# Issuing eleven of the bulk loads from ScalarE's DMA queue instead of SyncE's

## The chip, the cores and the metric

The kernel runs on one core of a Trainium2 chip. The metric is the device time of one execution in microseconds (us). A time is the median of the runs of that kernel; beside it stands the kernel before, run on the same chip in the same rounds. Of the engines only three matter: SyncE (SP in the profile) and ScalarE (ACT), which issue DMA transfers here and do nothing else, and VectorE (DVE), which does all the arithmetic.

## The reference

```python
x = np.random.randn(8192, 8192).astype(np.float32)
return np.linalg.norm(x, ord=np.inf, axis=1)      # the largest |x| of each row
```

268 MB are read once and 8192 numbers are written.

## The kernel before

48 of each partition's 64 rows are loaded in 24 bulk loads of two rows for each of the 128 partitions (64 KB a partition, 8.39 MB a load). Three buffers take turns, so load n+3 waits until reduction n has read its buffer. The last 16 rows, the tail, come in 31 smaller loads. I count loads and reductions from 0 throughout: the twelve loads of the first half are 0 to 11.

```python
    sbuf = ctx.enter_context(tc.tile_pool(name="sbuf", bufs=BUFS))     # BUFS = 3
    # ... (cut)
    def absmax(o, i):
        nc.vector.reduce_max(out=o, in_=i, axis=X, apply_absolute_value=True)

    for a in range(A):                       # A = 6
        for n in range(G):                   # G = 4: 24 bulk loads
            t = sbuf.tile([P, W + PAD], F32, tag="t")          # W = 16384
            nc.sync.dma_start(out=t[:, :W], in_=x_b[a, n])
            absmax(
                r_bulk[:, a, n * B : (n + 1) * B],
                t[:, :W].rearrange("p (b c) -> p b c", b=B),
            )
    nc.scalar.dma_start(out=out_b, in_=r_bulk[:])
    # ... (cut: the tail, 31 loads on nc.sync, each reduced as it lands)
    nc.at_finalize(start_first_load_early)   # SyncE's first load goes ahead of the start barrier
```

## Time and profile before

| | before |
|---|---|
| time, median of 3 | 628.22 us |
| span of the profiled run | 626.0 us |
| DVE busy | 552.9 us (88%) |
| read from HBM (the chip's main memory) | 268.44 MB, 429 GB/s over the span |

From the profile page of the kernel before, parts 1 and 2 (in the rows of digits each digit is the busy share of one fortieth of the span, in tenths):

```profile
span 626.0 us, 199 instructions
DVE 552.9 (88%) x64; POOL 0.2 (0%) x4
DVE  0588988889988889888898888988889999999998
DMA  9999999999999999999999999999999999999997
```

The DMA engines are busy in every slice. DVE has a little room until the last quarter, and almost none after it.

The timeline of the kernel before, cut to the start, the middle and the end of the bulk (start, duration, engine, line, operation, count; in brackets the idle time before it and what ended it):

```profile
22.00 17.22 DVE L139 TENSOR_REDUCE r_bulk<-t 128x2 f32<-128x16384 f32 x1 [21.02 <-DMA t<-in_x_dram]
41.27 17.22 DVE L139 TENSOR_REDUCE r_bulk<-t 128x2 f32<-128x16384 f32 x1 [2.06 <-DMA t<-in_x_dram]
...
234.67 17.22 DVE L139 TENSOR_REDUCE r_bulk<-t 128x2 f32<-128x16384 f32 x1 [2.14 <-DMA t<-in_x_dram]
254.02 17.22 DVE L139 TENSOR_REDUCE r_bulk<-t 128x2 f32<-128x16384 f32 x1 [2.13 <-DMA t<-in_x_dram]
273.32 17.22 DVE L139 TENSOR_REDUCE r_bulk<-t 128x2 f32<-128x16384 f32 x1 [2.07 <-DMA t<-in_x_dram]
292.69 17.22 DVE L139 TENSOR_REDUCE r_bulk<-t 128x2 f32<-128x16384 f32 x1 [2.15 <-DMA t<-in_x_dram]
...
466.68 17.22 DVE L139 TENSOR_REDUCE r_bulk<-t 128x2 f32<-128x16384 f32 x1 [2.14 <-DMA t<-in_x_dram]
```

A reduction starts every 19.33 us ((466.68 − 22.00) / 23), takes 17.22 us, and is preceded by about 2.1 us of waiting for its load. So the pace is that of the loads: 8.39 MB in 19.33 us, 434 GB/s.

From the same profile, the longest wait of SyncE's own queue (us in total, times, longest), the issue of load 14 in the timeline, and two lines of the DMA issues (the last number is the median time from issue to landing):

```profile
SPq L144 <- DVE r_bulk L139: 361.6, 21, 17.2
...
251.92 0.33 SPq L144 DMA_DIRECT2D t<-in_x_dram  x1
...
t<-in_x_dram SPq DMA_DIRECT2D x24, 40.7
out_dram<-r_bulk ACTq DMA_DIRECT2D x1, 24.0 KB, 60.4
```

SyncE mostly waits for buffers. A load is issued 21.4 us before the load ahead of it has landed (load 14: issued at 251.92, load 13 landed at 273.29), so it queues behind a whole load before it moves (the first packet of load 14 starts at 272.11). I call this time the **lead** of a load: from its issue to the landing of the load ahead of it. The store of r_bulk is only 24 KB but needs 60.4 us to land: on every engine its 48 packets of 32 B stand between packets of the loads, nearly all of them one at a time (in the order of the packet records, read as described below).

### The profile page before, as it was taken

To read this page: it belongs to the slowest core of one execution; us is meant where nothing else is said; L and a number is where in the kernel's file an instruction comes from. 1 tells how busy PE (TensorE), PEld (TensorE's weight loads), DVE (VectorE), ACT (ScalarE), POOL (GpSimd) and SP (SyncE) were. 2 spreads that over 40 slices of the span, in tenths; PEclk is the share of its full clock that TensorE was granted. 3 is DMA by queue.
4 is the path that set the end of the run, shared out by engine and by line. 5 is a ranking of instruction groups with operands and counts; after the bars stand their busy time and mean duration, and the time that the engine had idled before them with its cause. 6 is when DMAs were issued, how large, how long until landed. Compare 5 with 4: busy or idle time off the path is not lost.

```text
span 626.0 us, 199 instructions
## 1 busy us (share of the span) xinstructions
DVE 552.9 (88%) x64; POOL 0.2 (0%) x4
## 2 busy tenths in 40 slices
DVE  0588988889988889888898888988889999999998
POOL 0000000000000000000000000000000000000000
DMA  9999999999999999999999999999999999999997
GB/s 402 469 402 452 419 452 419 452 419 448 423 435 435 427 444 410 461 402 469 402 469 402 469 402 465 406 452 419 452 422 410 443 432 430 423 431 426 427 424 308
DMA packets 8994, 268.49 MB, mean 429 GB/s; under 512 B 1952, under 2 KB 1952, under 8 KB 3104
## 3 DMA queue, kind: packets, MB, share of 16 engines
q1 hardware_dynamic: 8064, 268.44, 99.4%
q10 hardware_dynamic: 928, 0.03, 0.1%
q14 instruction: 2, 0.02, 0.0%
HBM read 268.44 MB, written 0.03 MB: 429 GB/s over the span
## 4 chain that ended last, share of the span: by engine, by line
DMA 67%; DVE 29%; another core or an unknown queue 4%; SPq 0%; issue 0%
DMA t<-in_x_dram 67%; DVE r_bulk L139 22%; DVE part L139 5%; DVE t L139 1%; DVE r_fin L139 0%; SPq L157 0%; DVE r_tail L139 0%
## 5 line engine op out<-in xcount | busy, mean ns | idle before, releaser
L139 DVE TENSOR_REDUCE r_bulk<-t 128x2 f32<-128x16384 f32 x24 | 413.3, 17220 | 69.6 <-DMA t<-in_x_dram 69.6
L139 DVE TENSOR_REDUCE part<-t 128x1 f32<-128x8192 f32 (+18 forms) x31 | 130.4, 4274 | 0.8 <-DMA t<-in_x_dram 0.6
L139 DVE TENSOR_REDUCE t<-t 128x1 f32<-128x1152 f32 (+3 forms) x6 | 7.9, 1387 | 0.0
L139 DVE TENSOR_REDUCE r_fin<-t 128x1 f32<-128x1030 f32 x1 | 1.2, 1227 | 0.0
L136 DVE MEMSET part<- 128x60 f32 x1 | 0.1, 108 | 0.9 <-PEq L194 0.9
L139 DVE TENSOR_REDUCE r_tail<-part 128x15 f32<-128x60 f32 x1 | 0.2, 216 | 0.0
L194 POOL MEMSET const-uint8-127<- 128x1 uint8 x1 | 0.1, 102 | 0.0
L194 POOL MEMSET const-bfloat16-1.0<- 128x1 bf16 x1 | 0.1, 101 | 0.0
L194 POOL MEMSET const-float32-0.0<- 128x1 f32 x1 | 0.1, 98 | 0.2 <-issue 0.2
L194 POOL MEMSET const-float32-1.0<- 128x1 f32 x1 | 0.1, 98 | 0.0
## 6 DMA issues: line engine op xcount, KB each, us to landing
t<-in_x_dram SPq DMA_DIRECT2D x1, 6720.0 KB, 40.4
t<-in_x_dram SPq DMA_DIRECT2D x2, 3264.0 KB, 26.2
t<-in_x_dram SPq DMA_DIRECT2D x3, 2048.0 KB, 28.7
t<-in_x_dram SPq DMA_DIRECT2D x1, 6144.0 KB, 40.6
t<-in_x_dram SPq DMA_DIRECT2D x1, 5760.0 KB, 35.3
t<-in_x_dram SPq DMA_DIRECT2D x3, 1664.0 KB, 32.2
t<-in_x_dram SPq DMA_DIRECT2D x2, 2432.0 KB, 32.4
t<-in_x_dram SPq DMA_DIRECT2D x1, 4352.0 KB, 43.0
```

What stands on the lines that cost most here:

```text
L136: nc.vector.memset(part[:], 0.0)
L139: nc.vector.reduce_max(out=o, in_=i, axis=X, apply_absolute_value=True)
L194: nc = _bacc.Bacc("TRN2", target_bir_lowering=False, num_devices=1)
```

## The change

Issuing a DMA occupies a queue for about 0.33 us (0.328, the median of the 24 bulk loads before), and SyncE issues nearly all of them while ScalarE is idle. The intent is to share the issuing: loads 1 to 11 move to ScalarE; load 0 and everything from load 12 on stay on SyncE.

```diff
     for a in range(A):
         for n in range(G):
             t = sbuf.tile([P, W + PAD], F32, tag="t")
-            nc.sync.dma_start(out=t[:, :W], in_=x_b[a, n])
+            i = a * G + n
+            queue = nc.scalar if 1 <= i < A * G // 2 else nc.sync
+            queue.dma_start(out=t[:, :W], in_=x_b[a, n])
             absmax(
```

## The prediction

> **What bounds the kernel now.** The DMA engines. The DMA row of the page stands at 9 tenths in 39 of 40 slices, at 429 GB/s over the span. In the timeline the 24 bulk reductions start 19.33 us apart and take 17.22 us each; before each, DVE idles about 2.1 us. So a load of 8.39 MB takes 19.33 us (434 GB/s), and DVE has 2.1 us of slack per tile. SyncE's issue takes 0.33 us; its queue waits 361.6 us for DVE to free buffers. A load takes 40.7 us from issue to landing: it queues for about one whole load before it moves.
>
> **What the change does.** It saves SyncE 11 hidden issues: worth 0. It adds no bytes and no DVE work. It puts loads 1 to 11 (counting from 0) on a second ring. [...] the 24 KB store of r_bulk on ScalarE's queue, 48 packets per engine, took 60.4 us to land beside the loads, as if each packet waited for a load packet. So landings move in two places, where both rings hold loads:
>
> 1. Start. Load 0 is issued at 0.00 us, load 1 at about 0.8. Today load 0 lands at 22.0 and load 1 at 41.3. Now they alternate: load 0 lands at 36 to 41, load 1 still at 41. DVE begins some 17 us late. With 2.1 us of slack per tile it has caught up at about tile 8. Meanwhile loads are still issued 7 to 18 us before the previous one ends, so the engines stay fed.
>
> 2. Hand-over. Load 12 (SyncE) is issued when reduction 9 ends, about 213.2 us, and is ready as load 11 (ScalarE) begins to move, near 214.5. They share: both land near 251 to 254 instead of 234.7 and 254.0. Reduction 11 then ends at 269 to 271.5 and only then is load 14 issued, while load 13's last packets end at 272 to 273. An issue into idle engines needs 1.0 to 1.7 us to its first packet (load 0). So here the engines may run dry for 0 to 1 us: the only growth of the critical path. DVE catches up again by about tile 20, before the tail (466 us on), which is unchanged and has DVE at 9 tenths.
>
> **Time.** 628.2 + about 0.5 = 628.7 us; 8 in 10 between 627.8 and 630.5. Faster by over 2%: 0.01; within 2%: 0.97; slower: 0.02.
>
> **What would show it.** Right: total DVE busy unchanged (553 us), DMA row still 9 throughout at 428 to 429 GB/s; two DVE idles, about 38 us at the start (21.0 today) and 17 to 20 us before reduction 11, and then reductions back to back with no wait for some 8 tiles after each; reduction 23 starts within 1.5 us of 466.7. A lower DMA row or a DVE wait near 290 us would show the dry spell.
>
> **What would make it wrong.** Two rings at once moving less than one (over the 80 us where both are live, 3% is 2.4 us), or more; unequal sharing, which would starve load 11 past 254 us, and then load 14 is issued later and the engines idle for as long.

## The result, and the profile after

The changed kernel took 630.94 us (630.47 to 632.19, 6 runs) against 628.23 us (6 runs): a ratio of 1.0045, 95% interval 1.0032 to 1.0058. By the 2% rule that is the same; it is also 2.7 us slower, clear of noise, and above the predicted range. Ratios are the mean time of one kernel's fast runs over that of the other's of the same rounds, so not quite the ratio of the medians quoted.

The profile page of the changed kernel, the same lines:

```profile
span 628.3 us, 202 instructions
DVE 551.5 (88%) x64; POOL 0.2 (0%) x4
DVE  0059999999998880799999999988889999999998
DMA  9999999999999999999999999999999999999997
```

Its timeline, the same places:

```profile
0.80 194.13 ACTq L146 DMA_DIRECT2D t<-in_x_dram  x11
38.86 137.10 DVE L139 TENSOR_REDUCE r_bulk<-t 128x2 f32<-128x16384 f32 x8 [37.88 <-DMA t<-in_x_dram]
177.35 17.22 DVE L139 TENSOR_REDUCE r_bulk<-t 128x2 f32<-128x16384 f32 x1 [1.38 <-DMA t<-in_x_dram]
...
215.98 17.22 DVE L139 TENSOR_REDUCE r_bulk<-t 128x2 f32<-128x16384 f32 x1 [2.06 <-DMA t<-in_x_dram]
254.69 154.31 DVE L139 TENSOR_REDUCE r_bulk<-t 128x2 f32<-128x16384 f32 x9 [21.49 <-DMA t<-in_x_dram]
411.10 17.22 DVE L139 TENSOR_REDUCE r_bulk<-t 128x2 f32<-128x16384 f32 x1 [2.11 <-DMA t<-in_x_dram]
...
469.15 17.22 DVE L139 TENSOR_REDUCE r_bulk<-t 128x2 f32<-128x16384 f32 x1 [2.18 <-DMA t<-in_x_dram]
```

The course of events is the predicted one. DVE starts at 38.86 us instead of 22.00 and then makes eight reductions without a pause until it has caught up. It idles again for 21.49 us before reduction 11 (254.69 instead of 234.67) and catches up over nine more. But reduction 23 now starts at 469.15 instead of 466.68: 2.5 us have been lost, and not by DVE, which was waiting for loads again from 411 us on. The rows of tenths do not show the loss: the DMA row is the same digit for digit. The other sign that the prediction named, a wait of DVE near 290 us, does not appear either: DVE is still catching up then and reduction 13 starts at 288.95 us without a wait.

It has to be looked for at the hand-over. Load 14 waits for the buffer of load 11. In SyncE's part of the timeline it is issued at 271.94 us:

```profile
271.94 0.33 SPq L146 DMA_DIRECT2D t<-in_x_dram  x1
```

Load 13, ahead of it, landed at 273.96 by the trace's semaphore updates. So the lead of load 14 has shrunk from 21.4 us to 2.0.

The trace also records each DMA packet. A packet of a bulk load is 64 KB, as much as one partition gets; a load has 128, so 8 for each of the 16 engines, and one takes 2.418 us (median before). Chaining packets, each start to the end that it follows, gives for each engine the order of the packets of the two rings (by a ring I mean the packets of one queue at one engine; S: a packet of SyncE's ring, A: of ScalarE's). The chain is my own reading of the packet records, not a view of the profile:

```
first 41 us, all 16 engines:    S S A S A S A S A S A S A S A A A
                                load 0 is the eight S; the next A are load 1, the last begins load 2
from 215 us, 14 of 16 engines:  A S A S A S A S A S A S A S A S S
                                load 11 is the eight A; the first eight S are load 12, then load 13
load 11 on those engines:       last data packet ended 251.1 to 251.8 us
                                the 4-byte word that counts it as landed started 253.6 to 254.2 us
```

In these chains the rings take strict turns, one packet each. There is one thing in it that I had not reckoned with: a load has a packet of 4 bytes on its queue at each engine as well, after its data and 0.4 to 0.5 us ahead of one of the load's 16 semaphore updates (load 11). I take it for the word that raises the semaphore. In the chain it comes after one more packet of the other ring. All of load 11's data had been moved by 251.8 us, and on these engines the word started 2.4 us after the last packet; the last update came at 254.67, and DVE started at 254.69. Whether it was the turn that held the word, the traces do not tell.

Progress can be compared too: bytes moved up to a time, before minus after, divided by 434 GB/s. While two rings were live nothing was lost (0.05 us at 41 us; no growth from 214 to 254 us). The deficit grew by 0.7 us between 60 and 117 us, where packets took 2.44 to 2.57 us, by 0.8 us around 273 us, and by 0.3 us between 296 and 350 us, slow packets again. So the theory to test was: **the loss comes from load 14's short lead, not from having two rings.** The rivals were that two live rings move less; that moving work to ScalarE's queue costs in itself; and that DVE running without a pause slows the loads (the slow packets).

### The profile page after: what moved, and what is told of

Same layout as the page of the kernel before. It is cut to its first block, busy times and chain, and to the rows that moved or that the text cites. A ratio compares the mean times of both kernels' runs of the same rounds, so it can differ in the third digit from the quotient of the medians.

```text
span 628.3 us, 202 instructions
## 1 busy us (share of the span) xinstructions
DVE 551.5 (88%) x64; POOL 0.2 (0%) x4
## 4 chain that ended last, share of the span: by engine, by line
DVE 62%; DMA 32%; another core or an unknown queue 3%; issue 2%; SPq 0%
DVE r_bulk L139 47%; DMA t<-in_x_dram 32%; DVE part L139 14%; DVE t L139 1%; DVE r_fin L139 0%; SPq L159 0%; DVE r_tail L139 0%
```

## The experiments

All ran with 5 rounds. The diffs are against the changed kernel, or against the kernel before where said.

### 1. The change once more

No edit.

> The changed kernel once more, for a second trace and a narrower interval. In its first trace the lost time stood in three places: about 0.7 us of load progress between 60 and 117 us, where packets of 64 KB took 2.44 to 2.57 us instead of 2.418; 0.8 us at 273 us, where load 14 was issued 2.0 us before load 13 landed; about 0.3 us between 296 and 350 us, slow packets again. If the slow packets come from the order of work (DVE trailing its loads and never idling), they stand at the same places again and the time is 630.5 to 631.5 us. If they are passing noise, this trace has them elsewhere or not at all, and the 0.8 us at 273 us alone stays.

Measured: 631.28 us against 628.17, ratio 1.0050 (1.0037 to 1.0063). This trace has no slow packets between 60 and 117 us, and its progress is level with before (−0.01 us) until 270 us. Then it loses 1.5 us at load 14, and 0.8 us more between 295 and 360 us, where packets were slow. The early slow packets are therefore no fixed part of the change, and the loss at load 14 is what returns. Its lead was again 2.0 us (issued 271.31, load 13 landed 273.32).

### 2. The start of the change without the hand-over at load 12

```diff
-            queue = nc.scalar if 1 <= i < A * G // 2 else nc.sync
+            queue = nc.scalar if 1 <= i < 3 else nc.sync
```

> Loads 1 and 2 alone on ScalarE, all else on SyncE: the start of the change without its hand-over at load 12. Expected by the theory that a load issued too late is the cost: load 0 lands at 38.8 us, DVE is 17 us late and has caught up by reduction 8; load 3 goes to SyncE at 56 us, some 4.5 us before load 2 ends, so its sharing is short and no load is issued later than 3 us before the previous one lands; time 628.2 to 629.0, and 0.7 us of that only if the slow packets at 60 to 117 us come back. Rival, that two live rings cost throughput: about half of the loss of 2.7 us, 629.5.

Measured: 627.92 us against 628.17, ratio 0.9999 (0.9985 to 1.0012), a little below what I expected. Its timeline:

```profile
38.93 137.10 DVE L139 TENSOR_REDUCE r_bulk<-t 128x2 f32<-128x16384 f32 x8 [37.95 <-DMA t<-in_x_dram]
...
466.68 17.22 DVE L139 TENSOR_REDUCE r_bulk<-t 128x2 f32<-128x16384 f32 x1 [2.13 <-DMA t<-in_x_dram]
```

DVE begins 17 us late and reduction 23 nevertheless starts at 466.68 us, exactly as before. The shared start is free.

### 3. The hand-over without the shared start

```diff
-            queue = nc.scalar if 1 <= i < A * G // 2 else nc.sync
+            queue = nc.scalar if i < A * G // 2 else nc.sync
```

The helper that pulls the first load ahead of the barrier was set to ScalarE, so load 0 still goes early.

> Loads 0 to 11 all on ScalarE (load 0 still issued ahead of the barrier), so that the start has one ring only and the hand-over at load 12 stays. Expected: DVE starts at 22.0 us as before, no slow packets before 214 us, load 11 lands at 254, load 14 is issued about 2 us before load 13 lands, the engines run dry for about 0.8 us on average there; time 629.5 to 630.5, the larger part of the loss. Rival, two live rings cost throughput: 629.5 too, but then lost evenly between 214 and 254 us and not at 273.

Measured: 630.86 us against 628.17, ratio 1.0048 (1.0035 to 1.0060): the whole loss, a little above what I expected. Reductions 11 and 23 in its timeline:

```profile
254.13 137.10 DVE L139 TENSOR_REDUCE r_bulk<-t 128x2 f32<-128x16384 f32 x8 [21.48 <-DMA t<-in_x_dram]
...
469.48 17.22 DVE L139 TENSOR_REDUCE r_bulk<-t 128x2 f32<-128x16384 f32 x1 [2.15 <-DMA t<-in_x_dram]
```

Nothing grew from 214 to 254 us (0.16 to 0.19 us), so the rival of slower rings falls; 1.9 us were lost between 270 and 285 us. Load 14's lead was 2.0 us. With twelve loads on ScalarE's queue alone the progress was 0.16 us behind at 214 us, 0.13 us of it because load 0 was issued at 0.13 instead of 0.00, so the queue itself is not slower.

### 4. One ring, with DVE delayed on purpose

Against the kernel before; the repeats give the same result:

```diff
+            if a * G + n == 11:
+                late = r_bulk[:, a, n * B : (n + 1) * B]
+                absmax(late, t[:, :2048].rearrange("p (b c) -> p b c", b=B))
+                absmax(late, t[:, :W].rearrange("p (b c) -> p b c", b=B))
```

> One ring only: the kernel before, with reduction 11 followed by two repeats of itself (2048 and 16384 columns, same result, about 19.4 us of DVE), so that DVE falls back by as much as in the hand-over, and load 14 is issued about 2 us before load 13 lands with no second ring at all. If the late issue is the cost: load 14 lands about 1.5 to 2.1 us later than the 292.67 us of before, and the time is 629.5 to 630.5 us, as in the run with the hand-over alone. If it takes two rings to lose time: 628.2 us, since DVE catches up before the tail.

Measured: 630.83 us against 628.17, ratio 1.0044 (1.0032 to 1.0057), again a little above what I expected. The profile has all bulk loads on SyncE, and load 14 issued at the same point as in the changed kernel:

```profile
0.00 428.92 SPq L144 DMA_DIRECT2D t<-in_x_dram  x24
...
271.79 0.33 SPq L144 DMA_DIRECT2D t<-in_x_dram  x1
...
469.33 17.22 DVE L139 TENSOR_REDUCE r_bulk<-t 128x2 f32<-128x16384 f32 x1 [2.14 <-DMA t<-in_x_dram]
```

The last line is reduction 23: 469.33 us, against 469.15 in the changed kernel and 466.68 before. One ring, the same lateness, the same loss. This is the run that settles that two rings are not needed: a lead of 2 us is enough (1.8 us here). Not all of the loss falls at load 14, though. In this trace that load landed 1.8 us later than before (294.51 against 292.67), and some 0.8 us more were lost after 295 us in slow packets, whose cause is open (see below); in run 3, whose trace has no slow packets there, load 14 alone landed 2.8 us late (295.48).

### 5. The hand-over two loads earlier

```diff
-            queue = nc.scalar if 1 <= i < A * G // 2 else nc.sync
+            queue = nc.scalar if 1 <= i < 10 else nc.sync
```

> Loads 1 to 9 on ScalarE, load 10 onwards on SyncE: the same change with its hand-over two loads earlier, just as DVE is catching up. Loads 9 and 10 still share the engines for some 35 us, as 11 and 12 did, and DVE again idles about 19 us. Estimate from the durations in the traces (19.33 us a load, 17.14 us a reduction, packets alternating): load 9 lands near 213 instead of 196, load 12 is issued about 4.6 us before load 11 lands instead of 2.0, later loads earlier still. By the theory that only the lead of the issue counts, nothing is lost: 627.9 to 628.6. If the sharing or the 20 us idle of DVE were the cost, 630 to 631 as before.

Measured: 628.25 us against 628.05, ratio 1.0003 (0.9991 to 1.0016). The timeline shows that the sharing and the long idle time are still there:

```profile
213.04 137.10 DVE L139 TENSOR_REDUCE r_bulk<-t 128x2 f32<-128x16384 f32 x8 [19.01 <-DMA t<-in_x_dram]
350.82 17.22 DVE L139 TENSOR_REDUCE r_bulk<-t 128x2 f32<-128x16384 f32 x1 [0.68 <-DMA t<-in_x_dram]
```

Load 9 landed at 213.02 us, as estimated, and the shortest lead after that was 4.5 us (load 12 issued at 230.29, load 11 landed at 234.79). Reduction 17, at 350.82, is where it was before (350.68). A DVE that idles 19 us and is then a reduction behind cost nothing here, where no lead got below 4.5 us.

### 6 to 10. How short is too short

Five doses of the delay of run 4, all on one ring and against the kernel before; only the small repeat differs (none, 1024, 3072, 4096, 8192 columns).

> One ring, DVE delayed at tile 11 by one repeat of the reduction (16384 columns, 17.1 us) without the small one: load 14 is issued about 4 us before load 13 lands instead of 1.8. By the theory of the lead no engine runs dry: 627.9 to 628.5. If a DVE that trails its loads and never idles for some 130 us were the cost (slow packets, say), 629.5 to 631 as with the larger delay.

> The same with 1024 columns more: lead about 2.9 us. The last packets of a load end 0.4 to 1.2 us before it lands, and first packets began 1.0 to 1.7 us after an issue in most engines, but 2.2 to 3.4 us in the slowest. So most engines are fed in time and a few late ones are dry: 628.2 to 630, between the leads of 4 and of 2.

> The same with 4096 columns: load 14 is issued about when load 13 lands (lead -0.4 us, 2.2 us later than with 2048). All engines dry, so each further us of delay costs a us: 632.3 to 633.5, that is 1.5 to 2.5 us above the run with 2048 columns. Each engine pauses 2 to 3 us, and its first packet takes 3.0 to 3.3 us instead of 2.42.

> One ring, DVE delayed at tile 11 as in the runs of this kind before, here by 8192 columns more than one reduction: load 14 is issued about 4.6 us after load 13 has landed (4.3 us later than in the run with 4096 columns, 631.1 us). All 16 engines then stand idle together, and each us of lateness should cost a us: 635.0 to 635.9. Rival, that the loss levels off near 3 us as it seemed to between leads of 1.8 and -0.3: 631 to 632.

> The same with 3072 columns: lead about 0.7 us, between the run of lead 1.8 (630.83 us) and that of lead -0.3 (631.11 us). If some engines start late whenever the issue falls while packets of the load before are still moving (last packets end 0.4 to 1.2 us before the landing, so here most engines have just run out), the spread of the landing is between 0.8 and 1.5 us and the time again 630.8 to 631.3; if the loss simply grows with the delay, the same. This run is to see where the spread goes away.

Measured (run 9 in 4 runs, the others in 5), with run 4 and the two-ring runs among them. The lead and the last three columns are read from one trace each. "Pause" is the mean over the 16 engines between their last packet of load 13 and their first of load 14; "first packet" is that packet's mean duration; "spread" is the time from the first to the last of load 14's 16 counts:

| run | columns | lead us | time, before us | ratio | pause us | first packet us | spread us |
|---|---|---|---|---|---|---|---|
| before | – | 21.4 | 628.22 | – | 0.00 | 2.42 | 0.78 |
| 6 | none | 4.1 | 628.07, 628.05 | 0.9999 | 0.00 | 2.48 | 1.13 |
| 7 | 1024 | 2.9 | 629.76, 628.05 | 1.0027 | 0.08 | 2.69 | 1.89 |
| change, two rings | – | 2.0 | 630.94, 628.23 | 1.0045 | 0.25 | 3.00 | 1.68 |
| 1, two rings | – | 2.0 | 631.28, 628.17 | 1.0050 | 0.65 | 3.11 | 2.60 |
| 3, two rings | – | 2.0 | 630.86, 628.17 | 1.0048 | 0.86 | 3.25 | 2.12 |
| 4 | 2048 | 1.8 | 630.83, 628.17 | 1.0044 | 0.45 | 3.15 | 1.50 |
| 10 | 3072 | 0.8 | 630.45, 628.01 | 1.0039 | 1.11 | 2.99 | 0.81 |
| 8 | 4096 | −0.3 | 631.11, 628.05 | 1.0048 | 2.36 | 3.00 | 0.78 |
| 9 | 8192 | −4.5 | 635.12, 628.01 | 1.0112 | 6.62 | 2.91 | 0.76 |

Run 6 has DVE working without a pause for 154 us, as in the change, and its time is that of the kernel before, so that rival falls as well. From its timeline:

```profile
235.06 154.35 DVE L139 TENSOR_REDUCE r_bulk<-t 128x2 f32<-128x16384 f32 x9 [2.15 <-DMA t<-in_x_dram]
...
269.56 0.33 SPq L144 DMA_DIRECT2D t<-in_x_dram  x1
...
467.41 17.22 DVE L139 TENSOR_REDUCE r_bulk<-t 128x2 f32<-128x16384 f32 x1 [2.15 <-DMA t<-in_x_dram]
```

Reduction 23 starts 0.7 us later than before in this trace, which is of the slowest of the five runs; 0.3 us of it was lost before load 14, and one of the 16 engines took 3.41 us for its first packet of load 14. So a lead of 4 us is close to the edge: the loss begins between leads of 4.1 and 2.9 us. It has three parts that the last three columns show.

First the pause itself. Then the first packet of load 14 takes on average 2.9 to 3.25 us instead of 2.42 at leads of 2 us and less. The start of the kernel shows the same: its 16 first packets took 2.78 to 3.29 us. A pause is not needed for this. In the trace of the change 10 of the 16 engines went from load 13 to load 14 with less than 0.1 us between, and their first packets took 2.56 to 3.28 us all the same, on average 2.97. These ten started 1.15 to 1.62 us after the issue. In run 6 the engines did not pause either, but started 2.98 us or more after the issue, and 15 of 16 took 2.42 us. Why a first packet is slow when its load is issued so late is not shown. Third, at leads of 1.8 to 2.9 us the engines restart unevenly: in run 1 their first packets of load 14 began between 272.40 and 274.69 us, the last one 3.4 us after the issue, while in run 8, where all had stopped, they began between 274.66 and 275.26 us. The slowest engine sets when DVE can start (load 11 in the change: 16 counts from 251.83 to 254.67 us, reduction at 254.69), and the spread does not heal: in the change it is 1.40 us at load 23, before it is 0.77. I put that down to all engines being busy from then on (9 tenths in every slice of the DMA row but the last).

Hence the curve has a shelf. From run 8 to run 9 the loss grows by 4.05 us (3.06 to 7.11) for 4.15 us of lead: one for one. Extending that line to a lead of 2.0 gives an estimate of 0.7 us; measured were 2.7 to 3.1. My expectations missed this twice: run 8 was to take 632.3 to 633.5 us and took 631.11, because the even restart returns part of what the longer pause costs (load 14 landed 1.1 us later than in run 4, after a pause 1.9 us longer); run 10 was a little faster than expected, too. Why an engine that is still busy with load 13 at the issue begins the new load up to 3.4 us after the issue is not settled by these runs. Run 7 also lost more in its tail than the others: its load 23 landed 1.2 us later than before and its last store 2.0 us later.

### 11 and 12. Are turns counted in packets?

If so, the hand-over can be mended by giving load 12 smaller packets.

```diff
-            queue.dma_start(out=t[:, :W], in_=x_b[a, n])
+            cuts = [0, 4096, 8192, 12288, W] if i == A * G // 2 else [0, W]
+            for lo, hi in zip(cuts, cuts[1:]):
+                queue.dma_start(out=t[:, lo:hi], in_=x_b[a, n][:, lo:hi])
```

> The changed kernel with load 12 alone cut into four loads of 4096 columns on SyncE (16 KB a packet instead of 64 KB); all other loads and queues as in the change. In the traces of the change each engine alternates one packet of load 11 and one of load 12, and the word that counts load 11 as landed waits for one more packet of load 12, 2.4 us. If turns are counted in packets, whatever their size, load 11 now gets four fifths of each engine: 8 turns of 2.42 + 0.61 us, landed at about 239 to 240 instead of 254, reduction 11 starts there, load 14 is issued near 257 with a lead of 16 us, and nothing is lost: 627.9 to 628.7. If the rings share by bytes, load 11 still lands at 254 and the time stays 630.5 to 631.5.

Run 12 is the same with `cuts = [0, 256, W]`.

> The changed kernel with the first 256 columns of load 12 as a load of their own ahead of the rest (8 packets of 1 KB an engine). By packet turns these 8 small packets stand against the 8 packets of load 11, so load 11 lands at about 235 to 236, as in the kernel before, DVE keeps its pace, nothing is lost: 627.9 to 628.7. By bytes: load 11 at 254 and 630.5 to 631.5. A mend for one small load, if it works; faster than the kernel before it should not be, as the engines are then busy throughout in both.

Measured: run 11 took 628.64 us against 628.01, ratio 1.0010 (0.9998 to 1.0023); run 12 took 628.32 us, ratio 1.0005 (0.9991 to 1.0018). Reduction 11 in the timeline of run 11, and then of run 12:

```profile
240.25 51.47 DVE L139 TENSOR_REDUCE r_bulk<-t 128x2 f32<-128x16384 f32 x3 [7.04 <-DMA t<-in_x_dram]
```

```profile
234.96 17.22 DVE L139 TENSOR_REDUCE r_bulk<-t 128x2 f32<-128x16384 f32 x1 [2.51 <-DMA t<-in_x_dram]
...
466.67 17.22 DVE L139 TENSOR_REDUCE r_bulk<-t 128x2 f32<-128x16384 f32 x1 [2.13 <-DMA t<-in_x_dram]
```

At the sizes tried here, turns are counted in packets: with packets of 16 KB against it, load 11 landed at 240.22 us instead of 254.67; with eight packets of 1 KB an engine, at 234.94, within 0.3 us of the kernel before (234.65). The small excess of run 11 is mostly the passing kind: its progress fell 0.75 us behind up to 150 us, where its packets were slow as in the first trace of the change, and 0.2 us at the cut load. Run 12 keeps the change whole and takes its cost away. Neither beats the kernel before, and there is nothing for them to gain, because the DMA engines of that kernel are never without a packet in the bulk (in its trace 16 packets are under way at any time from 3 to 462 us).

## Why the prediction was right or wrong

**Right: what bounds the kernel, and that the issues saved are worth nothing.** DVE's busy time was 551.5 us after and 552.9 before, and runs 2 and 5 move 2 and 9 loads to the other queue with ratios of 0.9999 and 1.0003.

**Right: where landings move.** Predicted were a start of DVE near 38 us (38.86), eight reductions without a wait (8), an idle time of 17 to 20 us before reduction 11 (21.49, a little over), catching up by about tile 20 (reduction 20 starts at 411.10 after a wait of 2.11), no loss from two live rings (0.05 us over the first 41 us, none over the 40 of the hand-over). "Two rings at once moving less" and "unequal sharing", named as what could make it wrong, did not occur.

**Right: where the loss would arise.** The step "and only then is load 14 issued, while load 13's last packets end" is what runs 1, 3 and 4 show.

**Wrong: its size.** The step that failed is the term "So here the engines may run dry for 0 to 1 us: the only growth of the critical path", priced at 0.5 us. The measured growth was 2.7 us, later 3.1, and reduction 23, which was to start within 1.5 us of 466.7, started at 469.15. The mean pause was 0.25, 0.65 and 0.86 us in the three traces with the hand-over, inside the 0 to 1 us that I gave, though single engines paused for up to 2.6 us. But the pause is not the whole price:

- The first packet of load 14 takes 0.6 to 0.8 us longer (3.00 to 3.25 us instead of 2.42), on engines that hardly paused too. The first packets of the kernel before show that (2.78 to 3.29 us); I had read their start times for the prediction and left out their durations.
- DVE waits for a load's slowest engine. I reckoned with one engine for all 16. The spread of a load's landing rose from 0.78 us to between 1.7 and 2.6 at load 14, and stayed. In run 1, which has no earlier losses, load 14's last packets ended on average 1.5 us later than before, and the load, which waits for the slowest engine, landed 2.9 us later (295.55 against 292.67); the average is pause (0.65), first packet (0.69) and the slower second and third packets (0.17) together.
- The lead was at the short end of what I gave. Reduction 11 ended at 271.91 and 271.28 us in the two traces, against "269 to 271.5". Load 11's count came one more turn of 2.4 us after its data. Data that ended by 251.8 us would have let load 14 go 2.4 us earlier, with a lead of 4.4 us, and run 6 with 4.1 us loses nothing. This last step is argued from the packet records; no run takes away the waiting of the count alone.

The passing slow packets added about 0.7 us to the first trace (60 to 117 us). They are not part of the cause: of the kernels with the same order of work up to that point, run 11 had them too (0.75 us) and run 5 a few (0.2), and runs 1 and 12 did not. Those after 295 us came in the change and in runs 1, 4 and 8 (0.3, 0.8, 0.8 and 0.5 us) and not in runs 3, 7, 9 and 10. No trace without a lead under 4 us has them (before, 2, 5, 6, 11, 12), so they may belong to the cost of a short lead; what makes them is open. With them the first trace adds up, as an estimate: load 23 landed 2.47 us later than before, of which 0.7 us are the early slow packets, 0.8 the pause and the first packet at load 14, 0.3 the late slow packets and 0.6 the slowest engine being further behind the average.

## What to carry to other kernels

In this kernel, whose DMA engines were already busy, moving loads to a second queue added no bandwidth (427 GB/s over the span, 429 before), but it changed when loads land: by equal turns, counted in packets (load 0 at 38.84 us instead of 21.97, load 11 at 254.67 instead of 234.65), with the count of the finished load 11 coming a turn of 2.4 us later as well. So where a stream of loads changes queues, work out when each load lands and how early the next one is issued; here 4 us ahead was free in the median, and 2 us ahead cost 2.7 to 3.1 us, about as much as a load issued 0.3 us after the one ahead had landed (3.1 us). Two things took the cost away here: a small load put in front of the intruding one (run 12), and a hand-over at a point where the reader is behind (run 5).
